# Splitting 21 weight chunks ahead of time, into DRAM, in a hybrid decoder step

## The chip, the cores and the metric

The kernel runs on one core of a Trainium2 chip. The metric is device time in microseconds (us) of one execution; three runs of the kernel before have a median of 1935.28 us (1935.13 to 1935.48). The profile is of one further execution on the same core.

## The reference: what is computed

One layer of a decoder for 264 tokens (256 of a new sequence, 8 single tokens of eight older sequences), D = 2048, all in float32:

```python
x = x + 0.5 * swiglu(rmsnorm(x, n1), f1g, f1u, f1d)     # first feed-forward, D_FF = 5504
h = rmsnorm(x, nm)
proj = h @ w_in                                         # 2048 x 4864
o_att  = sliding-window attention with sinks (16 query heads, 4 key/value heads)
o_rwkv = RWKV-7 time mixing (16 heads of 64), a recurrence over the tokens
x = x + concat(o_att, o_rwkv) @ w_out                   # 2048 x 2048
x = x + 0.5 * swiglu(rmsnorm(x, n2), f2g, f2u, f2d)     # second feed-forward
return rmsnorm(x, final), and the new caches and states
```

## The kernel before, in words

**Matrix products from split numbers.** A float32 product is made from two rounded parts of each operand. A weight chunk is 128 rows by 512 columns (four 128 x 128 blocks, 256 KB). `chunk` (L134) loads it from DRAM into a buffer `raw` through SyncE's DMA queue (SP), ScalarE (ACT) rounds it into `hi`, and VectorE (DVE) writes the rest into `lo` = raw - hi. `gemm` (L145) then issues for each of the four blocks three matmuls of TensorE (PE) with 264 columns: hi by xh, hi by xl, lo by xh. So a chunk is 12 wide matmuls, and a full input tile of 2048 rows is four chunks, k0 = 0, 4, 8, 12. There are six `raw` buffers and four of each of `hi` and `lo` (`CH, NRAW, NHL = 4, 6, 4`, L28), so the DMA queue can be six chunks ahead of the split, and the split four chunks ahead of TensorE.

**Stages.** The first feed-forward (`first_ffn`, `ffn`) goes through 43 column blocks of the hidden width in six parts; for each block f it multiplies one gate tile and one up tile (2 x 4 chunks), and at the end of a part it multiplies the part's rows of the down weight. `ffn` can be given a generator `side`, which is advanced once before each block f from the second part on; the first feed-forward is given none. Then comes the mixing stage (`mixing_body`): 38 tiles of w_in through `win(t)` (L411), in the order of the table `SEQ`: two tiles for the small projections, then batches of six tiles (r, k and v of two head pairs), the four key and value tiles, query tiles, the last batch, the last query tiles. After each of a tile's chunks, `gemm` advances the tasks that are in flight (`tick`): `prep` and `chain` for the recurrence, `kvtask`, `attend` and the decode tasks. These issue small float32 matmuls on TensorE (PSUM tiles named `m`; the wide ones go to `acc`), and much small work on ScalarE, VectorE and GpSimd (POOL). Last in the stage is the product with w_out (64 chunks), and then the second feed-forward runs as the first.

**What sets the order.** A scheduler that simulates the engines' time places every instruction in its engine's queue; `high_priority` lets the chunks' loads and splits go ahead of other work as far as their buffers allow, and `keep_in_program_order` pins an instruction behind the one written before it. On the chip each queue runs in that order: an instruction that waits holds everything behind it on its engine, and a DMA that waits on SP's queue holds the DMAs behind it.

**The buffer `o`.** `blk("o", 8)` is a region of 8 x 320 float32 per partition. It holds scratch squares for the norms of the first feed-forward and the mixing stage (`Norm.rstd`, L210, reads them last, right after the first tile of w_in), and later the eight query tiles `ob[i]`.

Of the kernel before, what the change touches and what calls it, by code (L numbers as in the profile page):

```python
# [7 lines left out]
F32 = mybir.dt.float32  # L8
F32R = mybir.dt.float32r
AF = mybir.ActivationFunctionType  # L10
ALU = mybir.AluOpType
AX = mybir.AxisListType

P = 128
# [13 lines left out]
CH, NRAW, NHL = 4, 6, 4  # L28
NACC, NM = 3, 5
NH, NQ, NT, NLD = 16, 8, 16, 6  # L30
ROW = 320
# [14 lines left out]
ROWS = ((0, 96), (96, 96), (192, 72))  # L46
ALPHA = math.exp(-0.5)
LKV = 26
SEQ = [('b', 0), ('b', 1), ('b', 2), ('kv', 0), ('kv', 1), ('kv', 2), ('kv', 3), ('q', 0), ('q', 1), ('q', 2), ('q', 3), ('b', 3), ('q', 4), ('q', 5), ('q', 6), ('q', 7)]
PASS = [[0, 1, 2, 3], [8, 9, 10, 11, 12, 13, 14, 15], [4, 5, 6, 7]]  # L50
VG1, VGM, VG2, VGF = 0, 16, 32, 48
# [5 lines left out]
def body(tc, I, O):  # L57
    nc = tc.nc
    V, A, G, TE, SP = nc.vector, nc.scalar, nc.gpsimd, nc.tensor, nc.sync
# [3 lines left out]
    def uid(s):  # L63
        cnt[0] += 1
        return f"{s}{cnt[0]}"

    def tt(e, out, a, b, op):
        return e.tensor_tensor(out=out, in0=a, in1=b, op=op)  # L68
# [4 lines left out]
    def ts(e, out, a, s1, op0, s2=None, op1=None):  # L73
        k = {} if op1 is None else dict(op1=op1)
        e.tensor_scalar(out=out, in0=a, scalar1=s1, scalar2=s2, op0=op0, **k)
# [7 lines left out]
    def mm(out, lhsT, rhs, start=True, stop=True, **k):  # L83
        return TE.matmul(out, lhsT, rhs, start=start, stop=stop, **k)  # L84
# [16 lines left out]
    def spawn(g):  # L101
        tasks.append(g)
        return g
# [5 lines left out]
    with ExitStack() as ctx:  # L109
        cp = ctx.enter_context(tc.tile_pool(name="cp", bufs=1))  # L110
        sp = ctx.enter_context(tc.tile_pool(name="sp", bufs=1))
        wp = ctx.enter_context(tc.tile_pool(name="wp", bufs=1))
        pp = ctx.enter_context(tc.tile_pool(name="pp", bufs=1, space=bass.MemoryType.PSUM))
        dp = ctx.enter_context(tc.tile_pool(name="dp", bufs=1, space=bass.MemoryType.DRAM))
        cur = [None]

        def blk(tag, n, dt=F32):
            t = sp.tile([P, n * ROW + (16 if tag == "e" else 0)], dt, tag=tag, bufs=1, name=uid(tag))
            return [t[:, j * ROW:j * ROW + T] for j in range(n)]

        def pairs(*rows):
            return [(t[j], t[j - 1]) for t in rows for j in range(len(t) - 1, 0, -2)]

        def tmp(shape=(P, T), dt=F32):
            pool, n = cur[0]
            return pool.tile(list(shape), dt, tag="t", bufs=n, name=uid("t"))

        def acc():
            return pp.tile([P, 512], F32, tag="acc", bufs=NACC, name=uid("acc"))
# [4 lines left out]
        def chunk(src, n, e, ahead=True):  # L134
            w = n * P
            with tc.high_priority() if ahead else nullcontext():
                raw = wp.tile([P, CH * P], F32, tag="raw", bufs=NRAW, name=uid("raw"))
                hi = wp.tile([P, CH * P], F32R, tag="hi", bufs=NHL, name=uid("hi"))
                lo = wp.tile([P, CH * P], F32R, tag="lo", bufs=NHL, name=uid("lo"))
                SP.dma_start(raw[:, :w], src)  # L140
                A.copy(hi[:, :w], raw[:, :w])  # L141
                tt(e, lo[:, :w], raw[:, :w], hi[:, :w].bitcast(F32), ALU.subtract)
            return hi, lo

        def gemm(ps, src, xs, step=None, rng=None, ahead=True, ready=None):  # L145
            n = len(xs)
            for k0 in range(0, n, CH):
                k1 = min(n, k0 + CH)
                if rng and k0 not in rng:
                    continue  # L150
                hi, lo = ready or chunk(src[:, k0 * P:k1 * P], k1 - k0, V, ahead)
                for k in range(k0, k1):
                    xh, xl = xs[k]
                    c = slice((k - k0) * P, (k - k0 + 1) * P)
                    mm(ps[:, :T], hi[:, c], xh, k == 0, False)
                    mm(ps[:, :T], hi[:, c], xl, False, False)
                    big[0] = mm(ps[:, :T], lo[:, c], xh, False, k == n - 1)
                if step:
                    step()
# [76 lines left out]
        def ffn(nrm, xr, gu, dn, nxt, load, begin=None, side=None, ready=None, end=None):  # L236
            rstd = None
            f0 = 0
            for pi, nf in enumerate(PARTS):
# [70 lines left out]
                        nxt(o)  # L310
                f0 += nf

        def first_ffn(n2):
            def load(k0):
                return n1.split(xr[k0], True)

            def nxt(o):
                n2.split(xr[o])
                n2.square(xr[o])
                A.dma_start(xsp[o], xr[o])  # L320

            with tc.tile_pool(name="f1", bufs=1) as fp:
                cur[0] = (fp, NH)
                x0 = fp.tile([P, KD + T], F32, name="x0")
                A.dma_start(x0, I["x0"])
                n1 = Norm(VG1, pairs(*xs4), ob, gains=x0[:, 0:KD])
                xr = [x0[:, KD:]]
                at = load(0)
                with tc.issue_after(at.ins):
                    first = chunk(I["gu1"][0, 0][:, 0:CH * P], CH, V, False)  # L330
                for e, j0, j1 in ((A, 1, 2), (SP, 2, 4)):
                    xg = fp.tile([P, j1 - j0, T], F32, name=uid("x"))
                    e.dma_start(xg, I["xT"][:, j0:j1, :])
                    xr += [xg[:, j] for j in range(j1 - j0)]

                def more(q):
                    xg = fp.tile([P, 4, T], F32, tag="x", bufs=3, name=uid("x"))
                    tc.keep_in_program_order(A.dma_start(xg, I["xT"][:, q * 4:q * 4 + 4, :]))
                    xr.extend(xg[:, j] for j in range(4))

                ffn(n1, xr, I["gu1"], I["dn1"], nxt, load, more, None, first)

        def dec_state(fp, XR):
            n = 4
# [24 lines left out]
        def mixing_body(mx, n2, n3, XD, XR):  # L369
            def fix(shape, name):  # L370
                return mx.tile(list(shape), F32, name=name)
# [11 lines left out]
            keep = fix((P, NP), "keep")  # L383
# [24 lines left out]
            mixed = [None] * 16  # L408
            have = [False]

            def win(t):  # L411
                ps = acc()
                gemm(ps, I["win"][t], n2.xs, tick)
                if not have[0]:
                    n2.rstd(rs)
                    have[0] = True
                return ps
# [490 lines left out]
            act(sgl, sgl, AF.Tanh, scale=0.5)  # L908
            ts(G, sgl, sgl, 0.5, ALU.mult, 0.5, ALU.add)
            bat, att, bts, scores = [], [], [], []  # L910
            for kind, i in SEQ:
                if kind == "b":
                    bt = newbatch(i)
                    for k in range(BATCH[i]):
                        p = bt.p0 + k
                        x = [shifted(2 + 3 * p + j, tmp()) for j in range(3)]
                        spawn(prep(p, bt, k, *x))
                    bat.append(spawn(chain(bt)))
                    bts.append(bt)
                    if len(bat) == len(BATCH):  # L920
                        A.dma_start(O["sh"], shc)
                elif kind == "kv":
                    w, p = i // 2, i % 2
                    ps = win(LKV + i)
                    if w:
                        xs = (tmp(),)
                        with tc.high_priority():
                            tt(V, xs[0], ps[:, :T], rs, ALU.mult)
                    else:
                        xs = (kvb[p],)  # L930
                        kT[p] = xs[0]
                        with tc.high_priority():
                            tt(V, xs[0], ps[:, :T], rs, ALU.mult)
                    spawn(kvtask(w, p, xs))
                else:
                    ps = win(LKV + 4 + i)
                    q = ob[i]
                    with tc.high_priority():
                        stt(q, ps[:, :T], 0.125, rs, ALU.mult, ALU.mult)
                    att.append(spawn(attend(i, q)))  # L940
                    if i % 4 == 3:
                        scores.append(spawn(dec_scores(i // 4)))
                    if len(att) == 8:
                        att.append(spawn(dec_attend(list(att), scores)))
            n2.xs = None
            xr = blk("x1", 8) + blk("x0", 8)
# [13 lines left out]
            k0 = 0  # L960
            late = []
            more = blk("e", 2, F32R)
            n3.to = pairs(blk("y", 8, F32R))
            for pi, ks in enumerate(PASS):
# [3 lines left out]
                to = pairs(*(late + [xs4[1], more] if ks[0] > 7 else xs4[:1]))  # L968
# [27 lines left out]
        def second_ffn(n3, xr, XR):  # L996
# [6 lines left out]
            with tc.tile_pool(name="f2", bufs=1) as fp:  # L1003
# [70 lines left out]
                for e, q, o, n, r in ((V, SP, 0, 1, rp[:, :T]), (V, A, 1, 3, rp[:, :T]), (G, SP, 4, 4, rb), (V, A, 12, 4, rp[:, :T])):  # L1074
# [2 lines left out]
                    d = min(o, 8)  # L1077
                    q.dma_start(O["yT"][:, d:d + n, :], y)

        xsp = [dp.tile([P, T], F32, tag=f"xsp{o}", name=f"xsp{o}") for o in range(KD)]  # L1080
        xs4 = [blk(f"x{i}", 8, F32R) for i in (3, 2, 1, 0)]
        kvb, ob, yb = blk("kv", 6), blk("o", 8), blk("y", 8)
        n2, n3 = Norm(VGM, pairs(*xs4), ob), Norm(VG2)
# [107 lines left out]
```

## Time and profile before

| | |
|---|---|
| median of three runs | 1935.28 us |
| the profiled execution's own time | 1934.77 us |
| its span, first to last instruction | 1932.9 us |
| granted TensorE clock, mean | 0.998 |
| first feed-forward, until the first w_in split | about 0 to 742 us |
| mixing stage, to the last small matmul | about 742 to 1150 us |
| second feed-forward and end | about 1150 to 1933 us |

The profile's parts read as follows. Busy time is the time in which an engine executed; the times of PE overlap each other, since matmuls are pipelined and their ends are modelled. PEld are the weight loads of TensorE, which run beside its matmuls. A view by windows gives each engine's busy time, the number of its instructions, the granted clock and the DMA engines' share in a stretch of the span; a view by groups gives the busy time, the mean duration, and the idle time ahead of a group with what ended it; the view of waits names who waited for whom.

### The profile page before, as it was taken

What the parts mean: (1) busy time and instruction counts of PE and PEld (TensorE: products, weight loads), DVE (VectorE), ACT (ScalarE), POOL (GpSimd) and SP (SyncE); (2) the same over time, 40 slices, a digit from 0 to 9 for tenths busy, and PEclk for the clock granted to TensorE, in tenths of its full rate; (3) what the DMA queues carried; (4) which work ended last, traced back from release to release, by engine and by line L of the source; (5) the groups of instructions that cost most, each with busy time, mean ns of one, the idle gap of its engine ahead of it and who ended that gap; (6) DMA issues with size and microseconds to landing.
All of it is one profiled execution on the core that took longest, in us unless ns stands there. A gap on an engine that the chain in (4) does not pass through costs nothing.

```text
span 1932.9 us, 45519 instructions
## 1 busy us (share of the span) xinstructions
PE 1919.4 (99%) x17171; PEld 1897.1 (98%) x17171; DVE 1311.8 (68%) x2606; ACT 1023.7 (53%) x2034; POOL 260.1 (13%) x376
## 2 busy tenths in 40 slices
PE   9999999999999999999999999999999999999998
PEld 9999999999999999999989999999999999999998
DVE  5865555655556568889988977866666666666665
ACT  5644444444444457675657555644444444444446
POOL 0401101011010113222102100300101001010012
PEclk9999999999999999999999999999999999999999
DMA  7666666666666668555646656666666666666664
GB/s 241 178 192 196 185 195 195 183 192 177 190 183 180 188 181 238 177 165 153 176 120 165 210 155 183 175 188 188 189 195 195 186 192 189 194 195 184 193 181 150
DMA packets 218464, 357.27 MB, mean 185 GB/s; under 512 B 33516, under 2 KB 71804, under 8 KB 218244
## 3 DMA queue, kind: packets, MB, share of 16 engines
q1 hardware_dynamic: 211936, 346.02, 60.8%
q10 hardware_dynamic: 6308, 8.35, 1.4%
q8 instruction: 134, 2.20, 0.4%
q14 instruction: 86, 0.70, 0.1%
HBM read 346.67 MB, written 9.69 MB: 184 GB/s over the span
## 4 chain that ended last, share of the span: by engine, by line
PE 96%; DVE 1%; ACT 1%; issue 1%; DMA 0%; POOLq 0%; POOL 0%; ACTq 0%; DVEq 0%
PE acc L84 89%; PE m L84 6%; DVE lo L68 0%; ACT t L78 0%; ACT hi L141 0%; DMA x<-in_x 0%; DVE t L801 0%; DVE st L68 0%; DVE Xt L68 0%; DMA ld<-in_bias 0%; ACT BT L533 0%; ACT L78 0%; POOLq L1187 0%; DVE PT L68 0%; PE m L528 0%
## 5 line engine op out<-in xcount | busy, mean ns | idle before, releaser
L68 DVE TENSOR_TENSOR lo<-raw,hi 128x512 fp32r<-128x512 f32 (+1 forms) x1288 | 874.0, 682 | 510.4 <-ACT hi L141 486.9
L141 ACT CAST hi<-raw 128x512 fp32r<-128x512 f32 (+1 forms) x1288 | 776.8, 606 | 820.2 <-PE acc L84 745.2
L84 PE MATMUL acc<-x,hi 128*128 128x264 f32 x4840 | 893.4, 286 | 0.8 <-ACT hi L141 0.8
L84 PEld LDWEIGHTS acc<-x,hi 128*128 128x128 f32 x4840 | 750.1, 189 | 4.3 <-ACT hi L141 1.0
L84 PE MATMUL acc<-x,lo 128*128 128x264 f32 x2420 | 691.3, 286 | 0.2 <-DVE lo L68 0.2
L84 PE MATMUL acc<-h,hi 128*128 128x264 f32 x2752 | 495.0, 284 | 0.0
L84 PEld LDWEIGHTS acc<-x,lo 128*128 128x128 f32 x2420 | 457.2, 189 | 2.7 <-issue 0.7
L84 PEld LDWEIGHTS acc<-h,hi 128*128 128x128 f32 x2752 | 424.4, 189 | 0.0
L84 PE MATMUL acc<-h,lo 128*128 128x264 f32 x1376 | 387.8, 284 | 0.0
L84 PEld LDWEIGHTS acc<-h,lo 128*128 128x128 f32 x1376 | 259.2, 189 | 0.0
L68 POOL TENSOR_TENSOR t<-t,t 128x264 f32<-128x264 f32 x74 | 79.8, 1078 | 1096.1 <-DVE t L68 949.8
L84 PE MATMUL acc<-y,hi 128*128 128x264 f32 x648 | 122.7, 284 | 0.0
L84 PE MATMUL acc<-o,hi 128*128 128x264 f32 x648 | 120.1, 284 | 0.0
L84 PE MATMUL acc<-kv,hi 128*128 128x264 f32 x582 | 109.8, 285 | 0.0
L84 PEld LDWEIGHTS acc<-y,hi 128*128 128x128 f32 x648 | 101.2, 189 | 0.1
L84 PEld LDWEIGHTS acc<-o,hi 128*128 128x128 f32 x648 | 100.1, 189 | 0.0
L71 DVE SCALAR_TENSOR_TENSOR x<-acc,x 128x264 f32<-128x264 f32 (+1 forms) x193 | 81.1, 425 | 24.3 <-PE acc L84 23.4
L84 PE MATMUL acc<-y,lo 128*128 128x264 f32 x324 | 92.0, 284 | 0.0
L84 PE MATMUL acc<-o,lo 128*128 128x264 f32 x324 | 92.0, 284 | 0.0
L84 PEld LDWEIGHTS acc<-kv,hi 128*128 128x128 f32 x582 | 89.9, 189 | 0.2
L68 DVE TENSOR_TENSOR t<-acc,t 128x264 f32<-128x264 f32 x156 | 67.4, 432 | 32.9 <-PE acc L84 32.9
L84 PE MATMUL acc<-kv,lo 128*128 128x264 f32 x291 | 82.9, 285 | 0.0
(307 smaller groups left out, 1592.5 us busy)
## 6 DMA issues: line engine op xcount, KB each, us to landing
raw<-in_gu SPq DMA_DIRECT2D x688, 256.0 KB, 3.4
raw<-in_dn SPq DMA_DIRECT2D x224, 256.0 KB, 2.9
raw<-in_win SPq DMA_DIRECT2D x152, 256.0 KB, 3.4
raw<-in_dn SPq DMA_DIRECT2D x160, 192.0 KB, 2.8
raw<-in_wout SPq DMA_DIRECT2D x64, 256.0 KB, 3.5
xsp<-x ACTq DMA_DIRECT2D x16, 132.0 KB, 3.4
x<-xsp SPq DMA_DIRECT2D x16, 132.0 KB, 4.2
ld<-in_sT SPq DMA_DIRECT2D x16, 128.0 KB, 3.6
```

The source lines that it names most:

```text
L68: return e.tensor_tensor(out=out, in0=a, in1=b, op=op)
L71: return V.scalar_tensor_tensor(out=out, in0=a, scalar=s, in1=b, op0=op0, op1=op1)
L84: return TE.matmul(out, lhsT, rhs, start=start, stop=stop, **k)
L141: A.copy(hi[:, :w], raw[:, :w])
```

## The change

For 21 tiles of w_in (t = 3 to 19 and 26 to 29, the list `AHEAD`) the last chunk, k0 = 12, is no longer split in the mixing stage. During the first feed-forward a generator `split_early` is advanced as `side`, once per block f. A step first stores the two parts of the chunk of the step before last to a DRAM tensor `kept`, then splits the chunk of the last step, then loads the next chunk, with two buffers each of `er`, `eh` and `el`. Its DMAs are on SP's queue, pinned in program order. In the mixing stage `win(t)` calls `fetch` for the next such tile: one DMA of 512 KB brings both parts into one of two slots of a tile in the buffer `o`, and `gemm` takes them in place of the chunk (`kept`). Since the buffer is used for that until tile 29, the query tiles get their `ob` when the first of them comes (after the four key and value tiles).

```diff
+AHEAD = [*range(3, 20), *range(26, 30)]
...
-        def gemm(ps, src, xs, step=None, rng=None, ahead=True, ready=None):
+        def gemm(ps, src, xs, step=None, rng=None, ahead=True, ready=None, kept=None):
...
-                hi, lo = ready or chunk(src[:, k0 * P:k1 * P], k1 - k0, V, ahead)
+                hi, lo = kept if kept and k1 == n else ready or chunk(src[:, k0 * P:k1 * P], k1 - k0, V, ahead)
...
+        def split_early(fp):
+            todo = [(I["win"][t][:, 12 * P:], [kept[i, :, e] for e in range(2)]) for i, t in enumerate(AHEAD)]
+            raw, parts, keep = [], [], tc.keep_in_program_order
+            while todo or raw or parts:
+                if parts:
+                    to, both = parts.pop()
+                    for d, x in zip(to, both):
+                        keep(SP.dma_start(d, x.bitcast(F32) if len(d.shape) == 2 else x.bitcast(F32).rearrange("p (k c) -> p k c", k=2)))
+                if raw:
+                    to, x = raw.pop()
+                    hi, lo = (fp.tile([P, CH * P], F32R, tag=n, bufs=2, name=uid(n)) for n in ("eh", "el"))
+                    A.copy(hi, x)
+                    tt(V, lo, x, hi.bitcast(F32), ALU.subtract)
+                    parts.append((to, (hi, lo)))
+                if todo:
+                    src, to = todo.pop(0)
+                    x = fp.tile([P, CH * P], F32, tag="er", bufs=2, name=uid("er"))
+                    keep(SP.dma_start(x, src))
+                    raw.append((to, x))
+                yield
...
-                ffn(n1, xr, I["gu1"], I["dn1"], nxt, load, more, None, first)
+                side = split_early(fp)
+                ffn(n1, xr, I["gu1"], I["dn1"], nxt, load, more, side, first)
...
+            early = {}
+
+            def fetch(i):
+                if i >= len(AHEAD):
+                    return
+                if not early:
+                    early[None] = sp.tile([P, 8 * ROW], F32, tag="o", bufs=1, name=uid("o"))
+                x = early[None][:, 16 + i % 2 * 8 * P:16 + (i % 2 + 1) * 8 * P]
+                with tc.high_priority():
+                    SP.dma_start(x.rearrange("p (e c) -> p e c", e=2), kept[i])
+                early[AHEAD[i]] = [x[:, e * CH * P:(e + 1) * CH * P].bitcast(F32R) for e in range(2)]
+
             def win(t):
                 ps = acc()
-                gemm(ps, I["win"][t], n2.xs, tick)
+                if t + 1 == AHEAD[0] or t in AHEAD:
+                    fetch(AHEAD.index(t) + 1 if t in AHEAD else 0)
+                gemm(ps, I["win"][t], n2.xs, tick, kept=early.get(t))
...
+                    ob = ob or blk("o", 8)
...
+        kept = dp.tile([len(AHEAD), P, 2, CH * P], F32, tag="kept", name="kept")
```

How this moves instructions is shown at three places. Numbers in names are buffers and tiles of the one build, and differ between the two builds.

The first is SP's DMA queue in the first feed-forward, in the second part of the hidden width. Before, it holds nothing but gate and up chunks there:

```order
L140 DMA raw407_2260<-in_gu1 128x512
L140 DMA raw410_2278<-in_gu1 128x512
L140 DMA raw413_2296<-in_gu1 128x512
L140 DMA raw416_2314<-in_gu1 128x512
L140 DMA raw419_2332<-in_gu1 128x512
L140 DMA raw422_2350<-in_gu1 128x512
L140 DMA raw430_2380<-in_gu1 128x512
L140 DMA raw433_2398<-in_gu1 128x512
```

Now two stores and a load come among the same eight chunks of a block:

```order
L141 DMA raw411_2269<-in_gu1 128x512
L141 DMA raw414_2287<-in_gu1 128x512
L141 DMA raw417_2305<-in_gu1 128x512
L141 DMA raw420_2323<-in_gu1 128x512
L141 DMA raw423_2341<-in_gu1 128x512
L141 DMA raw426_2359<-in_gu1 128x512
L321 DMA kept_90<-eh402_2227 128x512
L321 DMA kept_90<-el403_2228 128x512
L141 DMA raw437_2397<-in_gu1 128x512
L331 DMA er436_2395<-in_win 128x512
L141 DMA raw440_2415<-in_gu1 128x512
```

The load of `er436` stands one chunk behind the two stores; nothing else in the queue changed its place.

The second is ScalarE's queue at the same place. Before, and then now:

```order
L141 CAST hi408_2261<-raw407_2260 128x512
L141 CAST hi411_2279<-raw410_2278 128x512
L141 CAST hi414_2297<-raw413_2296 128x512
L298 CAST h369_2061<-t398_2216 128x264
L230 DMA out_vs<-in_cv 16x2032
L141 CAST hi417_2315<-raw416_2314 128x512
L141 CAST hi420_2333<-raw419_2332 128x512
L141 CAST hi423_2351<-raw422_2350 128x512
```

```order
L142 CAST hi412_2270<-raw411_2269 128x512
L142 CAST hi415_2288<-raw414_2287 128x512
L142 CAST hi418_2306<-raw417_2305 128x512
L299 CAST h369_2062<-t399_2219 128x264
L231 DMA out_vs<-in_cv 16x2032
L142 CAST hi421_2324<-raw420_2323 128x512
L325 CAST eh466_2555<-er436_2395 128x512
L142 CAST hi424_2342<-raw423_2341 128x512
```

The rounding of `er436` stands behind that of `raw420`, four chunks behind that of `raw411`, whose buffer `raw437` takes; VectorE's subtraction for it stands at the same place of VectorE's queue.

The third is SP's queue in the mixing stage, where the chunks of the tiles t = 6 to 8 are loaded. Before:

```order
L140 DMA raw2046_10949<-in_win 128x512
L140 DMA raw2052_10987<-in_win 128x512
L140 DMA raw2055_11005<-in_win 128x512
L140 DMA raw2058_11023<-in_win 128x512
L140 DMA raw2064_11052<-in_win 128x512
L140 DMA raw2067_11070<-in_win 128x512
L378 DMA ld2161_11581<-in_lw 128x256
L140 DMA raw2070_11088<-in_win 128x512
L140 DMA raw2073_11106<-in_win 128x512
L140 DMA raw2079_11132<-in_win 128x512
```

Now:

```order
L141 DMA raw2107_11144<-in_win 128x512
L141 DMA raw2110_11162<-in_win 128x512
L141 DMA raw2116_11204<-in_win 128x512
L444 DMA o2042_10770<-kept_90 128x1024
L141 DMA raw2119_11222<-in_win 128x512
L141 DMA raw2122_11240<-in_win 128x512
L141 DMA raw2128_11279<-in_win 128x512
L444 DMA o2042_10770<-kept_90 128x1024
L402 DMA ld2201_11713<-in_lw 128x256
L141 DMA raw2138_11312<-in_win 128x512
```

Each tile of the list has three loads in place of four, and among them stands one fetch; the first shown is for t = 5 and goes into the slot that t = 3 used, the second for t = 6 into that of t = 4. Over the whole stage the w_in loads on this queue go from 152 to 131, with 21 fetches of twice their size; ScalarE's roundings and VectorE's subtractions of weight chunks stay 1288 each over the kernel, 21 of them now in the first feed-forward. TensorE has the same 16154 matmuls. The places at which its queue goes over from wide matmuls to small ones or back number 214 before and 220 now.

More of the change, by code (lines that the diff above doesn't have):

```diff
@@ L339, in more @@
                     xr.extend(xg[:, j] for j in range(4))
-                ffn(n1, xr, I["gu1"], I["dn1"], nxt, load, more, None, first)
+                side = split_early(fp)
+                ffn(n1, xr, I["gu1"], I["dn1"], nxt, load, more, side, first)
+                assert next(side, side) is side
         def dec_state(fp, XR):
@@ L910, in mixing_body @@
             bat, att, bts, scores = [], [], [], []
+            ob = None
             for kind, i in SEQ:
```

## The prediction

> **What bounds the kernel now.** First the page's head and its costliest groups, for who is busy and what the removed work is:
>
> ```profile
> span 1932.9 us, 45519 instructions
> PE 1919.4 (99%) x17171; PEld 1897.1 (98%) x17171; DVE 1311.8 (68%) x2606; ACT 1023.7 (53%) x2034; POOL 260.1 (13%) x376
> L68 DVE TENSOR_TENSOR lo<-raw,hi 128x512 fp32r<-128x512 f32 (+1 forms) x1288 | 874.0, 682 | 510.4 <-ACT hi L141 486.9
> L141 ACT CAST hi<-raw 128x512 fp32r<-128x512 f32 (+1 forms) x1288 | 776.8, 606 | 820.2 <-PE acc L84 745.2
> ```
>
> TensorE is busy for 99% of the span. The splits wait for it, and hardly ever the other way round: ScalarE's idle time ahead of `hi` ends on a matmul (745.2 of 820.2 us). Since the share is a mean over stages, I read next the view by windows: the start, a piece of the first feed-forward, the mixing stage, and its densest 200 us.
>
> ```profile
> 0.00:50.00 50.00, 47.96 (x382) 47.45 (x383) 30.00 (x53) 28.73 (x54) 0.48 (x7) 1.00 0.74 240
> 100.00:150.00 50.00, 50.00 (x419) 50.00 (x418) 31.65 (x56) 22.13 (x36) 0.00 (x0) 1.00 0.67 193
> 742.00:1150.00 408.00, 404.97 (x4580) 384.52 (x4579) 347.74 (x950) 258.27 (x653) 75.00 (x182) 1.00 0.59 170
> 850.00:1050.00 200.00, 197.56 (x2456) 184.81 (x2455) 182.27 (x542) 125.88 (x326) 36.40 (x86) 1.00 0.54 151
> ```
>
> The columns are length, PE, PEld, DVE, ACT, POOL, granted clock, DMA share, GB/s. In the first feed-forward PE and PEld leave nothing free, VectorE has 18 of 50 us free. In the mixing stage VectorE is at 347.74 of 408 us, and at 182.27 of 200 in the middle; that is where the change takes work away. Yet PE idles only 408 - 404.97 = 3.0 us there. Who makes it wait is told by the waits of PE between 742 and 1150 us, the whole list:
>
> ```profile
> PE m L808 <- DVE PT L68: 1.2, 1, 1.2
> PE m L755 <- issue: 0.7, 1, 0.7
> PE m L84 <- ACT BT L533: 0.4, 1, 0.4
> PE m L84 <- ACT kr L544: 0.2, 1, 0.2
> PE m L84 <- DVE N L68: 0.2, 1, 0.2
> ```
>
> 2.7 us in five waits, all of small matmuls (`m`); none of a wide matmul for `hi` or `lo`. The five are single events behind attention and recurrence work, not a pattern.
>
> Is a busy PE at its peak there? The timeline shows it:
>
> ```profile
> 940.15 0.38 PE L758 MATMUL m<-C,t 128*128 128x128 f32 x2
> 940.29 0.37 PE L84 MATMUL acc<-x,lo 128*128 128x264 f32 x1
> 940.50 0.41 PE L84 MATMUL acc<-x,hi 128*128 128x264 f32 x2
> 940.74 0.28 PE L84 MATMUL acc<-x,lo 128*128 128x264 f32 x1
> 940.86 0.41 PE L84 MATMUL acc<-x,hi 128*128 128x264 f32 x2
> ```
>
> Wide matmuls start every 0.12 us (two from 940.50 to 940.74, one from there to 940.86), so a chunk of 12 is 1.44 us, and a tile of four 5.8 us. The first behind small work takes 0.21 us, 0.09 more; I take 0.2 us for an interruption, out and back. All of this is TensorE's own work, which the change leaves: the order has the same 16154 matmuls.
>
> **The change part by part.** *Removed from the mixing stage:* 21 roundings and 21 subtractions. Their prices in that stage and in the first feed-forward (groups with the shapes kept apart, VectorE and ScalarE from 742 to 1040 us, then both from 100 to 740 us):
>
> ```profile
> L68 DVE TENSOR_TENSOR lo<-raw,hi 128x512 fp32r<-128x512 f32 x150 | 103.1, 690 | 19.3 <-ACT hi L141 16.8 <-PE acc L84 1.6
> L141 ACT CAST hi<-raw 128x512 fp32r<-128x512 f32 x150 | 91.4, 616 | 59.4 <-PE acc L84 48.9 <-ACT t L426 2.5 <-DVE t L68 2.0
> L68 DVE TENSOR_TENSOR lo<-raw,hi 128x512 fp32r<-128x512 f32 x387 | 268.8, 695 | 225.5 <-ACT hi L141 217.3 <-PE acc L84 1.8
> L141 ACT CAST hi<-raw 128x512 fp32r<-128x512 f32 x386 | 239.4, 620 | 288.3 <-PE acc L84 283.5 <-DVE t L68 4.6
> ```
>
> VectorE gets 21 x 0.690 = 14.5 us back and ScalarE 21 x 0.616 = 12.9 us. On the path lies only what of the 2.7 us of PE's waits they end. Ends: nothing, and all 2.7 us. All but the 0.7 us name one of the two engines, but the longest is attention's (L808), behind query tiles, which are not in the list; I take half, -1.3 us.
>
> A sentence on a rule that says otherwise: the Trainium skill, page "Perfetto Trace Analysis", section "Identifying the Most-Contended Engine", holds that matmul busy time says little of how near TensorE is to its limit, and that the busy share of the weight loads says more. The trace bears the warning out in part, since PEld is busy for 384.52 us where PE shows 404.97; what that would give is the second rival below.
>
> *TensorE's order:* three interruptions more (220 changes between wide and small work for 214): 3 x 0.2 = +0.6 us. Ends 0 and, if each reordering also cost a wait like the longest before, some +2 us.
>
> *Added to the first feed-forward:* 21 x 0.695 = 14.6 us on VectorE and 21 x 0.620 = 13.0 us on ScalarE, in 21 blocks of 8 x 1.44 = 11.5 us. Cover is the 18 us of 50 that VectorE has free and the 28 of ScalarE. What could break the cover is the order of the queues. ScalarE's rounding of `er436` waits for its load, and all roundings of weight chunks stand behind it. The load leaves when `raw437` does, that is when the subtraction of `raw411` has freed the buffer; the rounding stands three chunks further on, 3 x 1.44 = 4.3 us later. Landing times, from the page's and the DMA view's issues (KB each, us to landing):
>
> ```profile
> raw<-in_gu SPq DMA_DIRECT2D x688, 256.0 KB, 3.4
> X<-sa SPq DMA_DIRECT2D x4, 512.0 KB, 4.8
> xsp<-x ACTq DMA_DIRECT2D x16, 132.0 KB, 3.4
> x<-in_xT ACTq DMA_DIRECT2D x3, 528.0 KB, 5.8
> ```
>
> Alone the load lands in 3.4 us, ahead of need. Behind its two stores, 256 KB each, I add 1.4 us for each (the step from 256 to 512 KB): 6.2 us, a wait of 1.9 us. ScalarE runs four chunks ahead of TensorE (four `hi` buffers), 5.8 us, of which the split itself takes 0.62 + 0.69; it can lose 4.4 us before a matmul waits, and loses 1.9 + 0.62 = 2.5. So 0, and at the bad end, with store and load one after the other (3.4 + 4.8 = 8.2 us, a wait of 3.9), 3.9 + 0.62 - 4.4 = 0.1 us for each of 21, +2 us. The stores themselves wait for splits done a block earlier, so they hold nothing. SP's wait is room, not need:
>
> ```profile
> SPq L140 <- DVE lo L68: 365.3, 382, 2.2
> ```
>
> from 100 to 740 us it stands waiting for a free buffer for 365.3 us. Traffic rises from 8 x 256 KB to 2.8 MB in 11.5 us, some 250 GB/s; the first row by windows shows 240 GB/s at a DMA share of 0.74, so there is room. Were all cover gone, 21 x (0.695 + 0.620) = 27.6 us.
>
> *Added to the mixing stage:* a fetch of 512 KB for each tile. It waits for the matmuls of the tile two before, which used its slot, and raw loads are queued behind it. From there to its own use TensorE has 3 + 1 + 3 chunks, 7 x 1.44 = 10.1 us and the small work between. It lands in 4.8 to 5.8 us by the rows above, so it has some 4.3 us to spare. The raw ahead of it in SP's queue needs the buffer of its tile's own first chunk, which is free at about the same time, so the queue is not held either. What may hold it is the block of the recurrence's DMAs:
>
> ```profile
> 822.17 0.42 SPq L513 DMA_DIRECT2D sa<-gm  x1
> 825.25 0.62 SPq L572 DMA_DIRECT2D X<-sa  x1
> 825.92 1.76 SPq L140 DMA_DIRECT2D raw<-in_win  x1
> ```
>
> SP stood from 822.6 to 825.25 us, 2.7 us, until the store had landed. Less than 4.3, so 0; the bad end is the third rival.
>
> *Sum*, against the profiled execution's own time, 1934.77 us (span 1932.9 and 1.9 around it): 1934.77 - 1.3 + 0.6 + 0 + 0 = 1934.1. The median of the runs lies 0.5 us above that execution, so I predict 1934.6 us.
>
> **The rivals.** A measurement of this kernel can tell about 0.2%, 3.9 us, from no change. *Small move, the forecast*: with all waits gone 1932.6, with the bad ends of order and rounding 1935.28 + 2 + 2 = 1939.3; within 0.2% but for the very end. Chance 0.80.
>
> *VectorE is the true bound* in the middle of the mixing stage, and PE's modelled ends hide it. For it: 182.27 of 200 us, and PEld with 200 - 184.81 = 15.2 us free there. Then VectorE's 14.5 us come back: 1920.8. Against it: the free time of the weight loads can be assigned. By tiles, 742 to 1150 us, wide matmuls (`acc`) and then small ones (`m`):
>
> ```profile
> 742.00:1150.00 408.00, 323.47 (x2445) 303.21 (x2444) 30.49 (x72) 0.00 (x0) 1.00 0.59 170
> 742.00:1150.00 408.00, 112.79 (x2135) 86.09 (x2135) 85.39 (x195) 60.17 (x197) 1.00 0.59 170
> ```
>
> The small ones run 112.79 us against 86.09 us of loads, 26.7 us more, which is more than the 23.5 us that PEld lacks. They stream longer than they load; no engine is waited for. Chance 0.07.
>
> *The kept chunk comes late*: slower. Place: the first of its 12 matmuls, in tiles near the `X<-sa` and `Xt<-sa` DMAs; it decides once SP holds a fetch, or a landing stretches, by over 4.3 us together. For it: SP's queue is in order, and a TensorE that waits holds all small work too. With three such places at 2 us each the time is 1941; with every landing at twice 5.8 us, 11.6 - 10.1 = 1.5 us for each of 21, 1967. Against it: a held TensorE frees no buffers, so the delay does not build up. Chance 0.10.
>
> *The rounding in the first feed-forward holds the chunk splits* (the two added instructions uncovered): 1935.28 + 27.6 = 1963. Chance 0.03.
>
> **How the numbers follow.** Forecast 1934.6 us. The likeliest case alone spans 1932.6 to 1939.3; the range goes a little past it downwards, 1931.5 to 1939.5, and leaves out most of the other three, 0.2 together. Faster by over 0.2% (below 1931.4) 0.07; within 0.80; slower (above 1939.2) 0.13.
>
> **What would show it.** Right: PE's windows in the first feed-forward stay at 50.00 of 50; the mixing stage keeps its length within 3 us while VectorE's busy time there falls by some 14 us and ScalarE's by 13; PE has no wait for `kept` chunks, and its waits there stay at 1 to 4 us. Wrong: a wait of PE `acc` on a DMA into `o`, or on ACT `hi` in the first feed-forward, or a mixing stage that is shorter by 5 us or more.

## The result, and the profile after

The changed kernel takes 1965.43 us in the median of six runs (1959.34 to 1969.88), the kernel before beside it 1935.38 us (1935.13 to 1936.87). The ratio is 1.0152, 95% interval 1.0141 to 1.0163: slower by 1.5%. The forecast of 1934.6 us, no change, was wrong, and the range (to 1939.5) missed it as well.

The profiled execution of the changed kernel is its fastest run, 1959.34 us, 24.6 us above the one of before. The head of its page, one group and two of its DMA issues (cut at the marks):

```profile
span 1957.2 us, 45584 instructions
PE 1929.2 (99%) x17171; PEld 1900.4 (97%) x17171; DVE 1305.8 (67%) x2606; ACT 1016.3 (52%) x2034; POOL 246.0 (13%) x376
...
L69 DVE TENSOR_TENSOR lo<-raw,hi 128x512 fp32r<-128x512 f32 (+1 forms) x1267 | 857.4, 683 | 460.3 <-ACT hi L142 439.1
...
er<-in_win SPq DMA_DIRECT2D x21, 256.0 KB, 5.9
kept<-eh SPq DMA_DIRECT2D x21, 256.0 KB, 4.7
```

The shares are as before, TensorE at 99%. As an average over the span they hide where 24 us went. The starts of the wide matmuls, counted through (6192 in the first feed-forward, 2592 in the mixing stage, 6192 in the second), cut the span into stages:

| stage, us | before | after |
|---|---|---|
| first feed-forward | 745.1 | 767.4 |
| mixing | 426.0 | 427.5 |
| second feed-forward | 744.1 | 744.1 |
| from the last wide matmul to the end | 11.8 | 12.0 |

So 22.3 us are lost in the first feed-forward and 1.5 in the mixing stage. The view by windows of the changed kernel shows a piece of the first feed-forward ahead of the first rounding, one among the roundings, then all blocks that have one, and the mixing stage with its dense middle (this stage begins 22 us later now):

```profile
100.00:150.00 50.00, 50.00 (x419) 50.00 (x418) 31.75 (x56) 21.90 (x36) 0.00 (x0) 1.00 0.67 199
300.00:350.00 50.00, 46.38 (x370) 44.70 (x369) 24.16 (x42) 22.57 (x43) 7.87 (x8) 1.00 0.73 234
130.00:480.00 350.00, 337.40 (x2733) 331.39 (x2732) 192.41 (x339) 160.40 (x296) 34.95 (x34) 1.00 0.71 222
764.00:1172.00 408.00, 403.64 (x4567) 382.61 (x4566) 336.21 (x926) 245.85 (x628) 61.66 (x183) 1.00 0.60 183
872.00:1072.00 200.00, 196.59 (x2440) 183.04 (x2438) 176.09 (x525) 119.75 (x313) 28.01 (x86) 1.00 0.53 157
```

and of the kernel before:

```profile
130.00:480.00 350.00, 350.00 (x2919) 350.00 (x2918) 202.65 (x344) 167.26 (x294) 38.00 (x36) 1.00 0.64 189
```

Between 130 and 480 us TensorE started 2733 matmuls where it had started 2919: 186 x 0.12 us = 22.3 us. That is the whole loss of the stage. VectorE and ScalarE did less there as well, not more: they waited. For what, the waits of the changed kernel between 130 and 480 us say: for PE the whole list, for ACT and DVE the line of the early split (for ACT only its ordinary wait for a free `hi` buffer is longer, 92.4 us in 129 waits):

```profile
PE acc L85 <- ACT hi L142: 8.2, 11, 1.4
PE acc L85 <- DVE lo L69: 4.2, 14, 0.3
...
ACT eh L325 <- DMA er<-in_win: 81.4, 21, 5.0
...
DVE el L69 <- ACT eh L325: 79.6, 21, 5.0
```

TensorE now waits for `hi` and `lo`, which it did nowhere between 130 and 480 us before. Behind that stands ScalarE, which 21 times of 21 stood before the rounding `eh` for the load of `er`, 3.9 us on average, and VectorE stood with it. One such block in the timeline of the changed kernel, SP's queue, then ACT, DVE and PE (in brackets the idle time ahead and what ended it):

```profile
311.81 0.43 SPq L321 DMA_DIRECT2D kept<-eh  x1
312.28 0.43 SPq L321 DMA_DIRECT2D kept<-el  x1
312.81 0.42 SPq L141 DMA_DIRECT2D raw<-in_gu  x1
313.28 1.13 SPq L331 DMA_DIRECT2D er<-in_win  x1
...
314.57 0.62 ACT L142 CAST hi<-raw 128x512 fp32r<-128x512 f32 x1 [0.47 <-PE acc L85]
320.23 0.62 ACT L325 CAST eh<-er 128x512 fp32r<-128x512 f32 x1 [5.04 <-DMA er<-in_win]
320.75 1.13 ACT L142 CAST hi<-raw 128x512 fp32r<-128x512 f32 x2
...
310.11 1.90 DVE L69 TENSOR_TENSOR lo<-raw,hi 128x512 fp32r<-128x512 f32 x3 [0.41 <-ACT hi L142]
...
320.88 0.69 DVE L69 TENSOR_TENSOR el<-er,eh 128x512 fp32r<-128x512 f32 x1 [4.97 <-ACT eh L325]
321.49 0.69 DVE L69 TENSOR_TENSOR lo<-raw,hi 128x512 fp32r<-128x512 f32 x1
...
320.13 0.28 PE L85 MATMUL acc<-x,lo 128*128 128x264 f32 x1
321.42 0.51 PE L85 MATMUL acc<-x,hi 128*128 128x264 f32 x2 [1.01 <-ACT hi L142]
322.23 0.39 PE L85 MATMUL acc<-x,lo 128*128 128x264 f32 x1 [0.30 <-DVE lo L69]
```

SP needs until 313.28 us to get to the load of `er`. ScalarE comes to its rounding at 315.19 us, 1.9 us later, and gets the data at 320.23. Meanwhile no weight chunk is rounded; TensorE uses up the four that are ready and stops at 320.25 us, first for `hi`, then for `lo`, which stands behind `el` on VectorE. Over the 21 blocks, from the issue of the load to ScalarE's readiness 2.1 us passed on average, and the wait was 3.9. The stall goes with the wait, block by block (stall: start-to-start times of matmuls above 0.2 us, less 0.12 us each):

| ScalarE's wait, us | 2.07 | 2.90 | 3.53 | 4.17 | 4.52 | 4.75 | 5.04 |
|---|---|---|---|---|---|---|---|
| TensorE's stall, us | 0 | 0 | 0.34 | 0.98 | 1.33 | 1.56 | 1.85 |

In 18 of the 21 blocks it is so: up to 3.2 us the wait costs nothing, and each further microsecond costs one. Three lose more: those at 268.8 and 398.9 us lose 0.50 and 0.76 us for waits of 3.08 and 3.33, and the one at 178.5 us loses 3.7 for a wait of 4.75, of which 1.5 in a stretch at half the clock (last section). Over all blocks the excess over 3.2 us is 18.4 us; the stalls, counted in this way, sum to 21.8 us.

### The profile page after: what moved, and what is told of

Read it like the earlier page. It is cut to its first block, busy times and chain, and to the rows that moved or that the text cites. A ratio compares the mean times of both kernels' runs of the same rounds, so it can differ in the third digit from the quotient of the medians.

```text
span 1957.2 us, 45584 instructions
## 1 busy us (share of the span) xinstructions
PE 1929.2 (99%) x17171; PEld 1900.4 (97%) x17171; DVE 1305.8 (67%) x2606; ACT 1016.3 (52%) x2034; POOL 246.0 (13%) x376
## 4 chain that ended last, share of the span: by engine, by line
PE 89%; DMA 5%; DVE 2%; ACT 2%; issue 1%; SPq 0%; POOLq 0%; POOL 0%; DVEq 0%; ACTq 0%
PE acc L85 82%; PE m L85 6%; DMA raw<-in_gu 4%; DVE lo L69 1%; DMA er<-in_win 1%; ACT hi L142 0%; ACT t L79 0%; DMA x<-in_x 0%; DVE t L839 0%; DVE x L72 0%; DVE PT L69 0%; ACT L79 0%; POOLq L1228 0%; DVE Xt L69 0%; DVE st L69 0%
## 5 line engine op out<-in xcount | busy, mean ns | idle before, releaser
L69 DVE TENSOR_TENSOR lo<-raw,hi 128x512 fp32r<-128x512 f32 (+1 forms) x1267 | 857.4, 683 | 460.3 <-ACT hi L142 439.1
L142 ACT CAST hi<-raw 128x512 fp32r<-128x512 f32 (+1 forms) x1267 | 758.3, 606 | 753.5 <-PE acc L85 668.5
L85 PE MATMUL acc<-x,hi 128*128 128x264 f32 x4672 | 867.4, 286 | 9.4 <-ACT hi L142 9.3
L85 PEld LDWEIGHTS acc<-x,hi 128*128 128x128 f32 x4672 | 725.2, 189 | 16.7 <-ACT hi L142 12.1
L85 PE MATMUL acc<-x,lo 128*128 128x264 f32 x2336 | 668.4, 286 | 3.9 <-DVE lo L69 3.8
L85 PEld LDWEIGHTS acc<-x,lo 128*128 128x128 f32 x2336 | 442.1, 189 | 8.4 <-DVE lo L69 7.2
```

## The experiments

Theory A: the time goes to this wait. Theory B: it goes to the added DMA traffic. Theory C: it goes to the two added instructions of each block. All three are judged by the length of the first feed-forward (745.1 us before, 767.4 changed). Edits are against the changed kernel.

**The load one block earlier, in three buffers.**

```diff
-                if raw:
-                    to, x = raw.pop()
+                if len(raw) > 1 or raw and not todo:
+                    to, x = raw.pop(0)
...
-                    x = fp.tile([P, CH * P], F32, tag="er", bufs=2, name=uid("er"))
+                    x = fp.tile([P, CH * P], F32, tag="er", bufs=3, name=uid("er"))
```

> As the change, but each chunk is loaded one block of the first feed-forward earlier (three buffers er for two), so that ScalarE finds it landed; the same loads, stores, roundings, subtractions and fetches. Theory A (ScalarE's in-order queue waits for the late load, 3.9 us on average, longer than the 3 us that the four hi buffers cover): the wait is gone, the first feed-forward is back at about 745 us, the whole at 1936 to 1938 us, with the 1.5 us of the mixing stage left. Theory B (the 11 MB of stores and 5.5 MB of loads slow the weight loads): the traffic is the same, so the time stays at 1955 us or more. Theory C (21 more roundings and subtractions are too much work there): stays at 1955 us or more.

Measured: 1946.34 us, ratio 1.0055 (1.004 to 1.007); first feed-forward 750.4 us. Most of the loss is gone, though not all. The waits of ACT from 130 to 480 us name another transfer:

```profile
ACT eh L325 <- DMA kept<-eh: 53.7, 18, 4.4
```

The load is hardly waited for any more (twice, 3.4 us in all), but the two-deep `eh` is: the rounding waits until the store of the block before has landed and frees it.

**The same work without the stores** (the mixing stage splits as before and fetches nothing).

```diff
-                        keep(SP.dma_start(d, x.bitcast(F32) if len(d.shape) == 2 else x.bitcast(F32).rearrange("p (k c) -> p k c", k=2)))
+                        pass
...
-                if t + 1 == AHEAD[0] or t in AHEAD:
-                    fetch(AHEAD.index(t) + 1 if t in AHEAD else 0)
-                gemm(ps, I["win"][t], n2.xs, tick, kept=early.get(t))
+                gemm(ps, I["win"][t], n2.xs, tick, kept=None)
```

> The first feed-forward loads and splits the 21 chunks as in the change but stores nothing, and the mixing stage splits them again as before (the early parts are left unused). Theory A: the load no longer stands behind two stores; it leaves some 1 us earlier and lands in about 3.5 us for 5.9, so ScalarE waits about 0.5 to 1.5 us, under the 3 us of cover: about 1935 us. Theory B: with a third of the added traffic left, a third of the loss, about 1943 us. Theory C: the work is all there, 1955 us or more.

Measured: 1936.32 us, ratio 1.0003 (0.9993 to 1.0013); first feed-forward 745.7 us. Its waits of ACT and its window, from 130 to 480 us:

```profile
ACT eh L325 <- DMA er<-in_win: 47.2, 21, 3.5
```

```profile
130.00:480.00 350.00, 349.93 (x2916) 349.71 (x2915) 215.82 (x364) 172.25 (x315) 39.69 (x36) 1.00 0.66 204
```

All 21 roundings and subtractions are there, ScalarE still waits 2.25 us for each load (it lands in 4.0 us now), and TensorE loses nothing. So the added work costs nothing, theory C falls; and a wait of this length fits into the cover.

**All the traffic without the split** (the chunk is loaded and stored twice as it is; the mixing stage splits as before).

```diff
...
-                    hi, lo = (fp.tile([P, CH * P], F32R, tag=n, bufs=2, name=uid(n)) for n in ("eh", "el"))
-                    A.copy(hi, x)
-                    tt(V, lo, x, hi.bitcast(F32), ALU.subtract)
-                    parts.append((to, (hi, lo)))
-                    x = fp.tile([P, CH * P], F32, tag="er", bufs=2, name=uid("er"))
+                    parts.append((to, (x, x)))
+                    x = fp.tile([P, CH * P], F32, tag="er", bufs=4, name=uid("er"))
...
```

> The first feed-forward loads the 21 chunks and stores each twice, as it came, with no rounding and no subtraction; the mixing stage splits them as before. All of the added traffic of the first feed-forward, nothing in ScalarE's and VectorE's queues. Theory A: about 1935 us. Theory B: about 1957 us or more. Theory C: about 1935 us.

Measured: 1935.47 us, ratio 1.0001 (0.9991 to 1.001); first feed-forward 745.0 us. Its window:

```profile
130.00:480.00 350.00, 350.00 (x2919) 350.00 (x2918) 202.66 (x344) 167.32 (x294) 38.01 (x36) 1.00 0.75 233
```

233 GB/s in place of 189, and not one matmul fewer. Theory B falls.

**The load ahead of the stores in each step** (the block that loads is moved to the top of the loop; the rounding takes the chunk loaded a step before, `if len(raw) > 1 or raw and not todo: to, x = raw.pop(0)`).

> As the change, but in each step the load stands ahead of the two stores in SP's queue instead of behind them; nothing else is different. Theory A: the load leaves about 1 us earlier and lands in 3.5 to 4.5 us, so ScalarE waits 0.5 to 1.5 us, under the cover: 1936 to 1939 us. Theory B: the same traffic, 1955 us or more. Theory C: 1955 us or more.

Measured: 1958.88 us, ratio 1.0121 (1.0106 to 1.0136); first feed-forward 766.2 us. Nearly nothing is won, where theory A as it stood let 1936 to 1939 us be expected. Its waits of ACT, DVE and PE from 130 to 480 us:

```profile
ACT eh L330 <- DMA kept<-eh: 44.4, 15, 3.8
...
DVE el L69 <- DMA kept<-el: 37.6, 8, 5.6
...
PE acc L85 <- DVE lo L69: 12.7, 13, 1.5
```

The stores, issued later, are what is late now: VectorE stands before `el` until the earlier `el` has landed in DRAM, and `lo` is held behind it. The same loss, by another wait in the same two queues.

**Four buffers for the parts, alone and with the earlier load.** Both are meant to remove the wait for the stores; the first has `bufs=4` for `eh` and `el` as its only edit, the second also the edit of the first experiment.

> As the change, with four buffers eh and el in place of two: the wait for a store of the buffer is out, the late load stays. Theory A in its first form (the load is what ScalarE waits for in the change): first feed-forward stays at 763 us or more, the whole at 1955 us or more. Second form (the stores hold the buffers as much as the load): first feed-forward under 757 us, the whole under 1950 us.

> As the run with the load one block earlier, and with four buffers eh and el in place of two, so that neither rounding nor subtraction waits for a load or for a store of its buffer. All work, traffic and fetches of the change are there. Theory A: first feed-forward 745 to 746 us, mixing stage 427 to 430 us, the whole 1936.5 to 1940 us. Rival (work and traffic together cost something of their own): first feed-forward 748 us or more.

Measured: 1967.46 us, ratio 1.0163 (1.0142 to 1.0183), first feed-forward 773.4 us; and 1963.24 us, ratio 1.0144 (1.0129 to 1.016), first feed-forward 770.7 us. The second was expected to remove the loss and did not. Its waits of ACT from 130 to 480 us:

```profile
ACT eh L325 <- DMA er<-in_win: 82.8, 21, 6.1
```

No wait for a store is left in either, and the load is late in both. With a free `eh` the scheduler placed the rounding earlier again, so that the load had a lead of 2.0 us (2.1 in the changed kernel), although it was issued a block "earlier" in the program. Buffers alone give no distance; the order of the queue sets it.

**The rounding pinned late.** So the last test leaves everything as in the kernel just shown (same loads and stores on SP in the same places) and ties the rounding, for the scheduler only, behind the last wide matmul of the block before:

```diff
-                    A.copy(hi, x)
+                    behind(A.copy(hi, x))
```

> As e7_no_waits (loads one block earlier, three load buffers, four buffers for the rounded parts), with one addition: the rounding of the 21 chunks is tied, in the order of the program only, behind the last wide multiplication of the block before, so that it stands about ten chunks later in the queues of ScalarE and VectorE; SyncE's queue has the same order of loads and stores as in e7. Theory A (the time goes to ScalarE's in-order queue standing before the rounding until its load has landed, and the three chunks of cover do not outlast that): with some 14 us of lead in place of 2.0 the mean wait at the rounding falls from 3.95 us to under 0.5, TensorE's stall over the 21 steps from 25 us to 0 to 3, the first feed-forward takes 745 to 748 us and the whole 1936 to 1941. Rival (the four extra buffers or three loads in flight cost, or the rounding's place in the queues does not matter): the first feed-forward stays at 765 to 771 and the whole at 1958 to 1963.

Measured: 1938.0 us, ratio 1.0012 (1.0003 to 1.0021); first feed-forward 745.0 us. Its window and its longest waits of ACT from 130 to 480 us (`issue`: the profile shows nothing that the engine waited for):

```profile
130.00:480.00 350.00, 350.00 (x2919) 350.00 (x2918) 213.69 (x363) 177.15 (x313) 38.00 (x36) 1.00 0.75 231
```

```profile
ACT hi L142 <- PE acc L85: 159.1, 218, 1.7
ACT hi L142 <- ACT eh L325: 4.8, 15, 0.6
ACT hi L142 <- issue: 3.8, 3, 1.3
```

All added work and all added traffic are there, each load leaves more than 30 us ahead, no rounding waits for one, and the 22 to 26 us of the first feed-forward are gone to the last matmul. Theory A is shown: one place in one queue was the whole loss of the stage.

**The mixing stage alone** (one chunk is split ahead of time, and every fetch brings that one).

> The mixing stage of the change with its 21 fetches and without the 21 splits, but the first feed-forward splits and stores one chunk alone; all fetches bring that one, so the results of the 21 tiles are not those of the reference. Theory A (the loss is the waits in the first feed-forward, and the mixing stage gains nothing, since TensorE waits for three small matmuls and not for splits): first feed-forward 745 to 746 us, mixing stage 427 to 430 us for 426.0 before, the whole 1936.5 to 1940 us. Rival (the mixing stage does gain by VectorE's 14.5 us once nothing else is disturbed): mixing stage under 424 us, the whole under 1934 us.

Measured: 1938.29 us, ratio 1.0012 (1.0002 to 1.0021); mixing stage 429.1 us against 426.0. So the part for which the change pays its price brings nothing; if anything it costs 2 to 3 us, of which a stretch at half the clock at 1062.8 us (last section) makes 1.7. That is what the kernel with the pinned rounding is left with as well (the same ratio), and no version here was faster than the kernel before.

**More cover: a fifth buffer of `hi` and `lo`** in the first feed-forward, taken from that stage's own pool:

```diff
+        hl = [wp, NHL]
...
-                hi = wp.tile([P, CH * P], F32R, tag="hi", bufs=NHL, name=uid("hi"))
-                lo = wp.tile([P, CH * P], F32R, tag="lo", bufs=NHL, name=uid("lo"))
+                hi = hl[0].tile([P, CH * P], F32R, tag="hi", bufs=hl[1], name=uid("hi"))
+                lo = hl[0].tile([P, CH * P], F32R, tag="lo", bufs=hl[1], name=uid("lo"))
...
+                hl[:] = [fp, 5]
...
```

> As the change, but in the first feed-forward hi and lo have five buffers each in place of four (in a pool of that stage), so that the split can be one chunk, 1.44 us, further ahead of TensorE. Theory A: ScalarE still waits some 4 us for each load, but the cover grows from about 3 to 4.4 us; TensorE loses at most a few tenths per block, first feed-forward 746 to 751 us, the whole 1937 to 1943 us. Rival (the weight loads themselves are late, since the raw buffers come free late): first feed-forward 760 us or more.

Measured: 1983.18 us, ratio 1.0231 (1.0207 to 1.0254); first feed-forward 792.9 us. TensorE's stall fell from 21.8 to 9.1 us, and yet the stage became 25 us longer, also in the blocks without any rounding: the wide matmuls started every 0.1263 us on average in place of 0.1200. One tile ahead of these buffers has 280 elements, 1120 bytes, which is 32 bytes over a multiple of 64. So the same again with that tile padded to 288 elements:

```diff
-                x0 = fp.tile([P, KD + T], F32, name="x0")
+                x0 = fp.tile([P, 288], F32, name="x0")[:, :KD + T]
```

> As e6_five_buffers (the rounded parts of the first feed-forward's weights in five buffers in place of four), with one tile ahead of them in the same pool padded from 280 to 288 elements, so that each buffer starts 32 bytes further on. Theory 1 (the slow pitch of the wide multiplications in e6, 0.127 us in place of 0.120, comes from where the buffers start): the pitch is 0.120 again, the 30 to 40 us of it are gone, and what is left is the stall: by theory A a fifth buffer gives 1.4 us more cover, and of the 21 waits of 3.9 us on average at most 9 us of stall stay; the first feed-forward takes 746 to 756 us and the whole 1937 to 1948. Theory 2 (the pitch comes from something else, such as which part of the memory the buffers lie in or five of them): it stays at 0.127, and the whole at 1975 to 1985. If theory A were wrong on the cover and the pitch right: about 767 and 1958.

Measured: 1965.08 us, ratio 1.0157 (1.0141 to 1.0172); first feed-forward 767.6 us. The windows from 550 to 575 us, past the last rounding, of before, of the unpadded and of the padded kernel:

```profile
550.00:575.00 25.00, 25.00 (x211) 25.00 (x210) 13.88 (x23) 12.62 (x23) 4.29 (x4) 1.00 0.60 183
```

```profile
550.00:575.00 25.00, 25.00 (x200) 25.00 (x199) 13.40 (x22) 12.02 (x22) 4.35 (x4) 1.00 0.56 174
```

```profile
550.00:575.00 25.00, 25.00 (x210) 25.00 (x210) 13.93 (x22) 12.62 (x22) 4.22 (x4) 1.00 0.60 184
```

200 matmuls in 25 us with PE "busy" throughout, and 210 with the pad, at the same granted clock: moving what lies behind that tile by 32 bytes changes the pitch. In the gate and up products only the weight buffers `hi` and `lo`, of what TensorE reads, lie behind it; there the pitch is 0.1262 us without and 0.1205 with the pad. The down products also read `h` from there, and keep 0.1233 us with the pad (0.1266 without); why is open. So the pitch is not quite back (0.1214 on average in this stage, 8.6 us over its 6143 plain steps). The stall is 13.9 us, above the 9 expected; so a fifth buffer takes about a third off the stall, not nearly all of it. Why it gives less than a chunk's 1.4 us was not found.

## Why the prediction was wrong, point by point

**The step that failed is the wait of the rounding in the first feed-forward.** The prediction had found the place: "ScalarE's rounding of `er436` waits for its load, and all roundings of weight chunks stand behind it". It then set a landing of 6.2 us against a lead of 4.3, a wait of 1.9, and a cover of 4.4 less the 0.62 of the rounding, that is 3.8 us of wait that would cost nothing.

- *The landing* of 6.2 us was right: 5.9 us.
- *The lead*, "three chunks further on, 3 x 1.44 = 4.3 us later", was 2.1 us on average. It was counted from queue positions, as if the load left at the moment in which the buffer came free. In the block shown the subtraction that frees the buffer (the last of the three from 310.11 us) ends at 312.01 us and ScalarE is ready at 315.19, 3.2 us later: the count ran from rounding to rounding, and a chunk's subtraction ends some 1.4 us after its rounding began. And SP reaches the load only at 313.28, another 1.3 us later, since two stores and one load stand ahead, about 0.5 us of issue each. This was the larger error: the wait is 3.9 us, not 1.9.
- *The cover* is 3.2 us of wait, not 3.8. The way from `eh` to the next `lo` was priced rightly, 0.62 + 0.62 + 0.69 = 1.93 us: from the start of `eh` at 320.23 to the end of `lo` at 322.18 us it is 1.95. But the cover was counted from the moment at which a `hi` buffer comes free, and the wait begins only after the rounding that fills it. In the block shown the buffer is free at 314.57 us, ScalarE is ready for `eh` 0.62 us later, and TensorE stops at 320.25: 5.68 - 0.62 - 1.95 = 3.1 us, close to the 3.2 that the blocks show.
- *The bad end* had a wait of 3.9 us, which is the mean that came, but by luck: it was 8.2 us of landing against 4.3 of lead, and the runs show 5.9 against 2.1. It was priced at "0.1 us for each of 21". By 3.2 us of cover the same wait costs 0.7 us, and since it varies from block to block between 1.65 and 5.0 us, the mean understates it: the excess is 18.4 us. A threshold had been applied to an average. The sign that the prediction had named for this, a wait of PE `acc` on ACT `hi` in the first feed-forward, is what the profile shows.

**The rival with the right place had the wrong mechanism.** "The rounding in the first feed-forward holds the chunk splits" gave 1963 us with a chance of 0.03, from the added instructions without cover, 27.6 us. The time is near, but the runs show the added instructions to cost nothing when the data are there (the pinned rounding, the kernel without stores). The loss is a load's landing, seen through a queue in order.

**"The stores themselves wait for splits done a block earlier, so they hold nothing"** was right for SP and wrong for the buffers: the next use of a two-deep `eh` or `el` waits until the store has landed. In the changed kernel this is hidden behind the load; it came up as soon as the load was moved.

**Traffic** ("so there is room") was right: 233 GB/s at no loss.

**TensorE sets the end of the mixing stage**: right. VectorE's busy time there fell from 347.74 to 336.21 us and ScalarE's from 258.27 to 245.85 (14 and 13 us were expected), and the stage did not become shorter. The rival "VectorE is the true bound", 1920.8 us, falls. The Trainium skill, page "Perfetto Trace Analysis", section "Identifying the Most-Contended Engine", would have TensorE judged by its weight loads; they show 382.61 of 408 us here, less than full as before, and still relief of VectorE bought nothing, as the assignment of that free time to small matmuls had said.

**The terms of -1.3 and +0.6 us** came out as +1.5 us together. The three waits that can be told apart in both kernels (`PT`, `BT`, `N`) are as long as before or longer, although VectorE has less to do. The waits of PE from 764 to 1172 us in the changed kernel:

```profile
PE m L846 <- DVE PT L69: 1.8, 1, 1.8
PE m L793 <- POOL dkv L789: 1.3, 1, 1.3
PE m L85 <- ACT BT L571: 0.9, 1, 0.9
PE m L85 <- DVE N L69: 0.2, 1, 0.2
```

4.2 us where there were 2.7. They are the same kind of event as before, attention and recurrence steps waited for by a small matmul. The small work goes in 104 pieces in place of 101, each followed by a slower first matmul. That the new order of TensorE's queue alone makes these waits longer is argued from that, not shown; no run isolated it.

**"The kept chunk comes late"** falls: 21 fetches of 512 KB land in 4.6 us (median), and no wait of TensorE in the stage names one.

Of the 24.6 us between the two profiled executions, 22.3 + 1.5 + 0.2 are placed by the stages. The median of the changed kernel lies 6 us above its profiled execution, and where these further microseconds go was not seen. One candidate is the half clock of the last section: the three runs near 1969 us have a mean granted clock of 0.994 to 0.996, the other three 0.997.

## What to carry to other kernels

Work that "fits into free time" of an in-order engine is free only if its data are there when its turn comes: price the transfer's landing against its true lead, which runs from the end of the issue of everything ahead in the DMA queue to the moment the engine arrives, not from positions in a queue. Compare the wait with the buffers' cover for each occurrence, not for the mean, and count on every engine of the chain what stands between the late item and the next matmul. More buffers do not make distance; the instruction that consumes has to be pinned late (here 25 us came back by pinning one instruction), and even so the relieved stage must be one that was waiting.

## What the runs showed of the hardware

**A short stall can cost the clock.** After some stalls of TensorE, with 0.9 to 2.1 us of idle time, a stretch of 3.4 us (once 6.8) ran at half the granted clock, which costs another 1.7 us for each 3.4. In the changed kernel, by windows around the first of the long stalls:

```profile
176.00:178.00 2.00, 2.00 (x19) 2.00 (x18) 0.00 (x0) 0.00 (x0) 0.00 (x0) 1.00 0.97 294
178.00:181.50 3.50, 1.81 (x13) 1.39 (x12) 2.24 (x4) 2.34 (x5) 0.00 (x0) 1.00 0.30 112
181.50:185.00 3.50, 3.50 (x19) 3.50 (x18) 1.90 (x3) 1.53 (x4) 0.00 (x0) 0.52 0.74 218
185.00:187.00 2.00, 2.00 (x18) 2.00 (x18) 1.13 (x2) 1.03 (x3) 1.17 (x1) 1.00 1.03 316
```

Wide matmuls start every 0.22 us in the third row, with PE shown busy all the time; only the clock column tells. The kernel before has none in its profiled execution; most of the other kernels had one to three, in the mixing stage too, and the kernel without the split one at 968.2 us, where nothing is fetched. In every case the last long stall, or the first of two, began 2.9 to 3.8 us ahead of the slow stretch. The kernel with the pinned rounding has two there, at 941.7 and 1064.6 us, and its mixing stage is 430.6 us long in place of 427.5. Not every stall of this length is followed by one. The Trainium skill, page "TensorE: Matmul & The Clock Gate", section "HAM oscillation — how this bites in real kernels", gives as the rule that TensorE should not idle for more than about 3.4 us; the trace shows the half clock of that section, but here a stall of 1.7 us (1.39 and 0.30) was enough, and 3.4 us is the length of the slow stretch.

**The start of a weight buffer can change the pitch of the matmuls**: 0.1262 us a piece in the gate and up products, in place of 0.1200, with buffers that start 32 bytes off a multiple of 64 (by the sizes ahead of them; the addresses themselves were not read), and 0.1205 with the pad, at an unchanged granted clock. Over the whole feed-forward the unpadded kernel loses 39 us by its pitch, more than the change itself cost.
